# A two-block forward pass on one core: where a modulation's partial sums are given out, and which engine makes the second token tile's columns

## The chip, the cores and the metric

One Trainium2 chip, one of its cores. The program runs once per measurement, and the metric is the device time of the execution in microseconds (us). All weights come from HBM in float32; products are split into a high and a low part (`w_hi`, `w_lo`, and the same for activations), so that one float32 product is three products on TensorE (PE).

## What is computed

Two transformer-like blocks over 256 tokens of 1024 features. What matters here is the first block:

```python
def first_block(x, c, ctx, ...):
    mod_x = (silu(c) @ ada_w + ada_b)[:, None, :]
    sh1, sc1, g1, sh2, sc2, g2 = split(mod_x, 6, axis=-1)
    hx = modulate(rmsnorm(x, norm1_g), sh1, sc1)
    hc = modulate(rmsnorm(ctx, norm1_g), csh1, csc1)
    # pooled channels and neighbourhood attention (8 heads, with context)
    x = x + g1 * (concat([pool_x, attn_x]) @ w_out)
    h2 = modulate(rmsnorm(x, norm2_g), sh2, sc2)
    x = x + g2 * peer(h2, peer_wq, peer_keys, peer_u, peer_v)
    return rmsnorm(x, final_g)

def peer(h, w_q, sub_keys, u, v):      # per block of 128 tokens
    q = (xb @ w_q).reshape(tb, 8, 2, 128)
    s = einsum('thpd,hpnd->thpn', q, sub_keys)
    sv, si = top_k(s, 16)              # then the 16 best of 256 pairs
    a = gelu(einsum('td,thkd->thk', xb, u[experts]))
    return einsum('thk,thkd->td', g * a, v[experts])
```

The second block (`second_block`: a gated recurrence, a sparse attention and an MLP) follows.

## The kernel before

One class, `Net`, builds the whole program. The calls of all four compute engines go through one helper, so nearly every instruction stands under line 226 (L226) in the profile and is told apart by its tiles: PE is TensorE, DVE VectorE, ACT ScalarE, POOL GpSimd, SP SyncE (whose DMA queue loads the weights, 512 KB a block, into `w_raw`; ACT makes `w_hi` of it and DVE `w_lo`).

The order of the instructions on each engine is made when the program is built. Large products (`gemm_rows`, `gemm_cols`, and `product` for w_out) call `pump()` (L472) between their matmuls; `pump` gives out pieces of side work (generators) whose inputs it thinks are ready by its own estimates of cost. `until(mark)` pumps until a named piece has been given out, whether ready or not. On the chip each engine runs its own list in that order and waits with semaphores.

Inside the first block, in order: the value product (`ga` with w_hi of wi_v), then for b = 0 to 3 a query product and a keys product (wi_q, 128x256 outputs, and wi_k, 128x512 outputs, both `gc` in the trace), with the wi_pool product (`ga`) ahead of b = 3. When a keys product ends, `ev_k` (L964) splits it into `khl` (ACT, then one DVE subtraction) and starts the neighbourhood attention of two heads (`neighbours`: scores `s` on PE, `s` and `m` on DVE, `pr` on ACT, `prT` on PE, `pT` on ACT, `o` on PE, `rows` on ACT, `oT` on PE). Then comes w_out: 96 products `wo` in four steps of 24 (k2 = 0 to 3), whose result, gated by g1, is added to x.

The modulation vectors g1, sh2, sc2 and g2 are made beside this work. `mod_steps` (L734) makes one vector out of eight DVE steps: each multiplies a 128x1024 block of ada_w by a column and adds it into `msum` (the first is a TENSOR_SCALAR, the other seven are SCALAR_TENSOR_TENSOR), and then PE adds up `msum` over its partitions (`mr` for g1; eight `mc`, 16 records in the trace, for the three others). So there are 32 DVE steps, in this order: g1, sh2, sc2, g2. The blocks are `w_ada`, 512 KB each, loaded on POOL's DMA queue through a `Feed` (L189) that asks for two blocks ahead of use and has three buffers; the load for a later step is issued when the step that last read that buffer is done. `pump` gives out one step whenever PE's planned time has gone on by `pause` = 2.4 (`self.tick`). A new sum first forces the sum ahead of it to its end (`until(("msum", n - 1))`, L741), which also gives out whatever side work stands before it. Deadlines force what is left: `upto(1)` after the loop over b, `upto(3)` after k2 = 2, n = 0 of w_out (L1015), `upto(4)` ahead of k2 = 3 (L1018).

After w_out the first block's end makes the normed, scaled and shifted columns of both token tiles (`normed`, transposes `tp`, `xt`, then the split `hh` and `hl`), the first query product `q`, its transposes `q0t` and `q0T`. `peer` (L1148) then makes the first scores `sc`, DVE chooses the experts (MAX8 and what follows), and POOL issues 256 indirect gathers (`uv`, 1 MB each, nine buffers). For each, DVE makes a dot product, ACT the gate and a diagonal matrix, PE the product `va` into the output.

Of the kernel before, what the change touches and what calls it, by code (L numbers as in the profile page):

```python
# [9 lines left out]
F32 = mybir.dt.float32  # L10
# [9 lines left out]
D = 1024  # L20
# [249 lines left out]
class Net:  # L270
    def __init__(self, tc, I, out):
# [8 lines left out]
        self.wait, self.active, self.marks, self.ahead = [], [], Marks(self), None  # L280
        self.tick, self.pause, self.next = None, 0.0, 0.0
        self.rings, self.running, self.steps, self.ended = {}, [], {}, set()
# [189 lines left out]
    def pump(self):  # L472

        if self.tick and self.busy["pe"] >= self.next:
            self.next = self.busy["pe"] + self.pause
            self.tick()
        low = lambda: self.low < min(self.used + 2, self.high) and self.done["w", self.low][0] + HOP <= self.busy["pe"]
        if low():
            self.low_part()
        self.flush()  # L480
        while True:
            if low():
                self.low_part()
            if not self.step():
                break
# [293 lines left out]
    def first(self):  # L779
# [4 lines left out]
        with ExitStack() as es:  # L784
# [162 lines left out]
            for b in range(4):  # L947
# [16 lines left out]
                def ev_k(a, qs=qs, kh=kh, kl=kl, b=b):  # L964
                    self.parts(kh, kl, a)
                    for e in range(2):
                        for tt in range(2):
# [4 lines left out]
                self.gemm_cols(xh, xl, "wi_q", b, T, ev_q)  # L972
                load_bias(2 * b + 1)
                self.gemm_cols(xh, xl, "wi_k", b, 512, ev_k)
            self.flush()
# [54 lines left out]
            self.prepare(-1)  # L1030
            self.r2 = [self.small.tile([128, 1], F32, name="gr", tag="gr") for t in range(2)]
            y = [pool.tile([128, D], F32, name="normed", tag="normed", bufs=2) for t in range(2)]

            def scale(tt):
                v = self.small.tile([128, 1], F32, name="gv", tag="gv")
                nc.vector.scalar_tensor_tensor(v, ss[tt][:, 1:2], 1.0 / D, ss[tt][:, 0:1], op0=ALU.mult, op1=ALU.add)
                nc.gpsimd.tensor_tensor(self.r2[tt], v, self.nhalf[:, :1], op=ALU.pow)

            def turn(tt):
                ps = []  # L1040
                for h in range(2):
                    p = self.pt("tp").rearrange("p (i t) -> p i t", i=4)
                    for i in range(4):
                        k = 4 * h + i
                        nc.tensor.transpose(p[:, i], y[tt][:, k * 128:(k + 1) * 128], self.ident)
                    ps.append(p)
                return ps

# [21 lines left out]
            square(0, 1)  # L1070
            self.normed_by(y[0], 0)
            evac(1, 1)
            ps = turn(0)
            xt = shift(ps[0], 0, nc.scalar)
# [9 lines left out]
            for h in range(2):  # L1084
                wh, wl = self.block("wq0", h, held=1 + h, more=-h)
                for i in range(4):
                    k, c = 4 * h + i, slice(i * 256, i * 256 + 256)
                    self.mm3(a, self.hh[:, k, :128], self.hl[:, k, :128], wh[:, c], wl[:, c], k == 0, k == 7)
            self.normed_by(y[1], 1)
            ps = turn(1)  # L1090
            q = pool.tile([128, 256], F32, name="q0", tag="gx", bufs=2)
# [5 lines left out]
            nc.scalar.activation(self.q0T, p[:, :256].rearrange("p (i t) -> p i t", i=2), AF.Copy)  # L1097
            for h in range(2):
                both(1, h, shift(ps[h], h, nc.vector), nc.vector)()

# [47 lines left out]
    def peer(self):  # L1148
# [3 lines left out]
        with ExitStack() as es:  # L1152
# [209 lines left out]
            self.offload = -99.0  # L1362
            self.ahead = pool, 6, self.loaded
            sc0 = self.res.tile([128, 256], F32, name="sc0")
            p = self.pt("sc")
            score(p, lambda i: self.q0T[:, i], 0, self.keys0)
            nc.scalar.activation(sc0, p[:, :256], AF.Copy)
            st["scored"].add((0, 0))
            q = queries()
            while st["gathered"] < 8:  # L1370
                advance(0.1, 0)
            token_rows(0)
            for _ in range(4):
# [768 lines left out]
```

## Time and profile before

| what | us |
|---|---|
| median of three runs (lowest, highest) | 1526.38 (1524.91, 1527.83) |
| the profiled execution, its own time | 1531.74 |
| its span in the trace | 1530.0 |
| busy: PE, DVE, ACT, POOL | 1350.7, 1038.0, 715.8, 291.7 |

The span is what the profiler's records cover; the profiled execution's own time is 1.74 us more, and 5.36 us above the median of the runs. An engine's busy time is a sum over stages with different limits: the first block up to w_out takes the first 200 us, the gathers run from 221 to about 875, and the second block takes the rest.

### The profile page before, as it was taken

The numbers are of one execution on the slowest core, as the hardware profiler recorded it, in microseconds if no ns is written. First come the engines' busy times: TensorE is split into PE (matmuls) and PEld (weight loads), VectorE is DVE, ScalarE is ACT, GpSimd is POOL, SyncE is SP. The second block draws the span as 40 slices with busy tenths as digits, with TensorE's granted clock in tenths as the row PEclk, the third lists the DMA queues.
The fourth block names the chain that finished last, engine by engine and source line by source line (L and its number), as shares of the span: only waits on it lengthen the run. The fifth ranks groups of instructions, "written<-read, shape, count | busy, mean of one in ns | idle before, by whom it ended". The sixth has DMA issues, their size and how long they took to land.

```text
span 1530.0 us, 18426 instructions
## 1 busy us (share of the span) xinstructions
PE 1350.7 (88%) x5972; PEld 913.4 (60%) x5972; DVE 1038.0 (68%) x2240; ACT 715.8 (47%) x1670; POOL 291.7 (19%) x338
## 2 busy tenths in 40 slices
PE   7999968988998788777787789999999999999996
PEld 3787755544543233222222258978788887998874
DVE  5665778777777778666654467767667667776454
ACT  3443335444554545444433356566633655444443
POOL 2110123333333333333333200000000100000000
PEclk9998979999999999999999999999999999999998
DMA  9665659999999999999999934532333365655652
GB/s 344 237 221 187 206 196 419 418 419 418 420 418 420 419 420 418 420 420 419 420 421 419 405 116 161 182 111 83 97 124 125 114 191 164 188 186 184 189 165 100
DMA packets 82080, 420.19 MB, mean 275 GB/s; under 512 B 10336, under 2 KB 12928, under 8 KB 49088
## 3 DMA queue, kind: packets, MB, share of 16 engines
q0 software_dynamic: 42672, 289.22, 46.5%
q1 hardware_dynamic: 39024, 129.52, 25.8%
q8 instruction: 48, 0.79, 0.2%
q14 instruction: 48, 0.39, 0.1%
q10 hardware_dynamic: 288, 0.27, 0.1%
HBM read 417.93 MB, written 1.05 MB: 274 GB/s over the span
## 4 chain that ended last, share of the span: by engine, by line
PE 45%; DMA 28%; DVE 11%; ACT 6%; issue 5%; POOL 1%; SPq 0%; DVEq 0%; POOLq 0%; ACTq 0%
DMA uv<-in_uv,ids 25%; PE ga L226 19%; PE gc L226 9%; PE va L226 6%; DVE uv L226 3%; DVE w_lo L226 2%; PE hA L226 2%; PE wo L226 2%; PE s L226 2%; ACT w_hi L226 1%; PE o L226 1%; PE no L226 1%; POOL uv L1305 1%; ACT L226 1%; ACT nP L226 1%
## 5 line engine op out<-in xcount | busy, mean ns | idle before, releaser
L226 PE MATMUL va<-uv,diag 128*128 128x512 f32 x1024 | 504.4, 623 | 112.4 <-ACT diag L226 109.8
L226 DVE SCALAR_TENSOR_TENSOR uv<-uv,xr 128x1024 f32<-128x1024 f32 x256 | 311.8, 1219 | 195.7 <-DMA uv<-in_uv,ids 179.5
L226 PEld LDWEIGHTS va<-uv,diag 128*128 128x128 f32 x1024 | 180.4, 193 | 384.9 <-ACT diag L226 237.2
L226 DVE TENSOR_TENSOR w_lo<-w_raw,w_hi 128x1024 fp32r<-128x1024 f32 x217 | 264.4, 1222 | 141.0 <-ACT w_hi L226 140.9
L226 ACT ACTIVATE w_hi<-w_raw 128x1024 fp32r<-128x1024 f32 x217 | 229.0, 1059 | 221.2 <-PE ga L226 138.0
L1305 POOL DMA_INDIRECT uv<-in_uv,ids x256 | 246.8, 964 | 414.5 <-PE va L226 296.3
L226 ACT ACTIVATE ga<-dots 128x1 f32<-128x1 f32 x256 | 51.9, 203 | 339.8 <-DVE uv L226 334.4
L226 PE MATMUL gc<-hh,w_hi 128*128 128x256 f32 x520 | 175.3, 337 | 0.0
L226 PE MATMUL gc<-hh,w_lo 128*128 128x256 f32 x520 | 150.0, 289 | 11.7 <-DVE w_lo L226 11.7
L226 PE MATMUL gc<-hl,w_hi 128*128 128x256 f32 x520 | 149.9, 288 | 1.4 <-DVE hl L226 1.4
L226 PEld LDWEIGHTS gc<-hl,w_hi 128*128 128x128 f32 x520 | 102.5, 197 | 15.9 <-issue 14.2
L226 PEld LDWEIGHTS gc<-hh,w_hi 128*128 128x128 f32 x520 | 102.9, 198 | 14.3 <-issue 14.3
L226 PEld LDWEIGHTS gc<-hh,w_lo 128*128 128x128 f32 x520 | 102.4, 197 | 12.3 <-DVE w_lo L226 12.3
L226 ACT ACTIVATE diag<-ident,c 128x128 f32<-128x128 f32 x256 | 102.8, 402 | 8.4
L226 PE MATMUL ga<-w_hi,hh 128*128 128x512 f32 x240 | 100.3, 418 | 0.9 <-ACT w_hi L226 0.7
L226 PE MATMUL ga<-w_lo,hh 128*128 128x512 f32 x240 | 95.5, 398 | 3.8 <-DVE w_lo L226 3.7
L226 PE MATMUL ga<-w_hi,hl 128*128 128x512 f32 x240 | 95.5, 398 | 0.4 <-DVE hl L226 0.4
L226 ACT ACTIVATE c<-ga,g 128x1 f32<-128x1 f32 x256 | 75.4, 295 | 8.3
L226 POOL TENSOR_TENSOR gr<-gv,nhalf 128x1 f32<-128x1 f32 x8 | 5.1, 634 | 313.6 <-DVE gv L226 313.6
L226 PEld LDWEIGHTS ga<-w_lo,hh 128*128 128x128 f32 x240 | 46.1, 192 | 13.2 <-DVE w_lo L226 5.2
L226 PEld LDWEIGHTS ga<-w_hi,hl 128*128 128x128 f32 x240 | 45.9, 191 | 11.4 <-DVE hl L226 1.3
L226 PEld LDWEIGHTS ga<-w_hi,hh 128*128 128x128 f32 x240 | 46.2, 192 | 10.3 <-ACT w_hi L226 1.1
(428 smaller groups left out, 2057.9 us busy)
## 6 DMA issues: line engine op xcount, KB each, us to landing
w_ada<-in_ada POOLq DMA_DIRECT2D x32, 512.0 KB
w_raw<-in_w_up SPq DMA_DIRECT2D x32, 512.0 KB, 3.8
w_raw<-in_w_down SPq DMA_DIRECT2D x32, 512.0 KB, 3.5
w_raw<-in_wq SPq DMA_DIRECT2D x18, 512.0 KB, 7.8
ring<-in_ada SPq DMA_DIRECT2D x16, 512.0 KB, 9.5
w_raw<-in_w_kv SPq DMA_DIRECT2D x12, 512.0 KB, 3.9
w_raw<-in_w_out SPq DMA_DIRECT2D x8, 512.0 KB, 4.3
uv<-in_uv,ids POOLq DMA_INDIRECT x256
```

Source lines behind the costliest of these rows:

```text
L226: r = call(out, *args, **kwargs)
L1305: tc.nc.gpsimd.indirect_dma_start(rows[i], None, I["uv"], bass.IndirectOffsetOnAxis(ap=ids[i % 16], axis=0))
```

## The change

Two edits. First, a flag `hold`: it is set when a keys product begins and cleared in `ev_k` when its result is split, and while it is set `pump` gives out no modulation step. Steps that would have been given out there come at a later `pump`, or at a deadline. Second, the columns of the second token tile are no longer made at the end of the first block. They are made in `peer` behind the first scores: both halves of `xt` and `hh` on ACT (before: all of it on DVE), and the two `hl` on DVE after the eighth gather has been given out. `s2` and `sh2` are handed over in `self.cols2`; the transposes became a method, `turn8`; the tiles take other tags, and `r2` lies in a longer-lived pool.

```diff
--- before.py
+++ after.py
@@ -278,7 +278,7 @@
         self.busy, self.done, self.dma = dict(pe=0.0, dve=0.0, act=0.0, pool=0.0), {}, 0.0
         self.nsums = 0
         self.wait, self.active, self.marks, self.ahead = [], [], Marks(self), None
-        self.tick, self.pause, self.next = None, 0.0, 0.0
+        self.tick, self.pause, self.next, self.hold = None, 0.0, 0.0, False
         self.rings, self.running, self.steps, self.ended = {}, [], {}, set()
         self.depth, self.margin, self.backlog, self.offload, self.force = 4, 0.4, 2.5, -9.0, [False]
 
@@ -471,7 +471,7 @@
 
     def pump(self):
 
-        if self.tick and self.busy["pe"] >= self.next:
+        if self.tick and not self.hold and self.busy["pe"] >= self.next:
             self.next = self.busy["pe"] + self.pause
             self.tick()
         low = lambda: self.low < min(self.used + 2, self.high) and self.done["w", self.low][0] + HOP <= self.busy["pe"]
@@ -963,6 +963,7 @@
 
                 def ev_k(a, qs=qs, kh=kh, kl=kl, b=b):
                     self.parts(kh, kl, a)
+                    self.hold = False
                     for e in range(2):
                         for tt in range(2):
                             k = 2 * b + e, tt
@@ -971,6 +972,7 @@
 
                 self.gemm_cols(xh, xl, "wi_q", b, T, ev_q)
                 load_bias(2 * b + 1)
+                self.hold = True
                 self.gemm_cols(xh, xl, "wi_k", b, 512, ev_k)
             self.flush()
             upto(1)
@@ -1028,23 +1030,14 @@
             for n in range(2):
                 product(n, 1, 3, *ws[n])
             self.prepare(-1)
-            self.r2 = [self.small.tile([128, 1], F32, name="gr", tag="gr") for t in range(2)]
-            y = [pool.tile([128, D], F32, name="normed", tag="normed", bufs=2) for t in range(2)]
+            self.r2 = [self.res.tile([128, 1], F32, name=f"r2{t}") for t in range(2)]
+            y = pool.tile([128, D], F32, name="normed", tag="normed", bufs=2)
+            self.cols2 = s2, sh2
 
             def scale(tt):
                 v = self.small.tile([128, 1], F32, name="gv", tag="gv")
                 nc.vector.scalar_tensor_tensor(v, ss[tt][:, 1:2], 1.0 / D, ss[tt][:, 0:1], op0=ALU.mult, op1=ALU.add)
                 nc.gpsimd.tensor_tensor(self.r2[tt], v, self.nhalf[:, :1], op=ALU.pow)
-
-            def turn(tt):
-                ps = []
-                for h in range(2):
-                    p = self.pt("tp").rearrange("p (i t) -> p i t", i=4)
-                    for i in range(4):
-                        k = 4 * h + i
-                        nc.tensor.transpose(p[:, i], y[tt][:, k * 128:(k + 1) * 128], self.ident)
-                    ps.append(p)
-                return ps
 
             def shift(p, h, engine):
                 xt = pool.tile([128, 4, 128], F32, name="xt", tag="pr", bufs=3)
@@ -1068,9 +1061,9 @@
             scale(0)
             evac(0, 1)
             square(0, 1)
-            self.normed_by(y[0], 0)
+            self.normed_by(y, 0)
             evac(1, 1)
-            ps = turn(0)
+            ps = self.turn8(y)
             xt = shift(ps[0], 0, nc.scalar)
             low = both(0, 0, xt, nc.scalar)
             square(1, 1)
@@ -1086,8 +1079,6 @@
                 for i in range(4):
                     k, c = 4 * h + i, slice(i * 256, i * 256 + 256)
                     self.mm3(a, self.hh[:, k, :128], self.hl[:, k, :128], wh[:, c], wl[:, c], k == 0, k == 7)
-            self.normed_by(y[1], 1)
-            ps = turn(1)
             q = pool.tile([128, 256], F32, name="q0", tag="gx", bufs=2)
             nc.scalar.activation(q, a, AF.Copy)
             p = self.pt("q0t")
@@ -1095,8 +1086,15 @@
                 nc.tensor.transpose(p[:, i * 128:(i + 1) * 128], q[:, i * 128:(i + 1) * 128], self.ident)
             self.q0T = self.res.tile([128, 2, 128], F32, name="q0T")
             nc.scalar.activation(self.q0T, p[:, :256].rearrange("p (i t) -> p i t", i=2), AF.Copy)
-            for h in range(2):
-                both(1, h, shift(ps[h], h, nc.vector), nc.vector)()
+    def turn8(self, y):
+        ps = []
+        for h in range(2):
+            p = self.pt("tp").rearrange("p (i t) -> p i t", i=4)
+            for i in range(4):
+                k = 4 * h + i
+                self.nc.tensor.transpose(p[:, i], y[:, k * 128:(k + 1) * 128], self.ident)
+            ps.append(p)
+        return ps
 
     def normed_by(self, y, tt):
         nc = self.nc
@@ -1361,14 +1359,29 @@
 
             self.offload = -99.0
             self.ahead = pool, 6, self.loaded
+            s2, sh2 = self.cols2
             sc0 = self.res.tile([128, 256], F32, name="sc0")
             p = self.pt("sc")
             score(p, lambda i: self.q0T[:, i], 0, self.keys0)
             nc.scalar.activation(sc0, p[:, :256], AF.Copy)
             st["scored"].add((0, 0))
+            y = pool.tile([128, D], F32, name="y1", tag="g2r")
+            self.normed_by(y, 1)
+            ps = self.turn8(y)
+            xts = []
+            for h in range(2):
+                xt = pool.tile([128, 4, 128], F32, name="xt", tag=("vg", "qT")[h], bufs=1 + h)
+                for i in range(4):
+                    k = 4 * h + i
+                    nc.scalar.activation(xt[:, i], ps[h][:, i], AF.Identity, scale=s2[:, k:k + 1], bias=sh2[:, k:k + 1])
+                nc.scalar.activation(self.hh[:, 4 * h:4 * h + 4, 128:], xt, AF.Copy)
+                xts.append(xt)
             q = queries()
             while st["gathered"] < 8:
                 advance(0.1, 0)
+            for h in range(2):
+                c = slice(4 * h, 4 * h + 4)
+                nc.vector.tensor_tensor(self.hl[:, c, 128:], xts[h], self.hh.bitcast(F32)[:, c, 128:], op=ALU.subtract)
             token_rows(0)
             for _ in range(4):
                 next(q)
```

What moves, engine by engine. The first place is DVE at the end of the second keys product (b = 1). One piece of the difference there (- is before only):

```order
 L226 TENSOR_TENSOR w_lo<-w_raw,w_hi 128x1024 x2
 L226 SCALAR_TENSOR_TENSOR qs<-gc,qs 128x256
-L226 SCALAR_TENSOR_TENSOR msum<-w_ada,sl,msum 128x1024 x2
 L226 TENSOR_TENSOR khl<-gc,khl 128x512
 L226 TENSOR_TENSOR s<-s,bias 128x256
```

The two steps of a sum that stood ahead of `khl` are gone from this place.

The second place is DVE in w_out, towards its end, down to g2's `mc`. Before:

```order
L226 RECIPROCAL rz<-z 128x1
L226 TENSOR_TENSOR w_lo<-w_raw,w_hi 128x1024
L226 TENSOR_TENSOR s<-s,bias 128x256
L226 TENSOR_REDUCE m<-s 128x1
L226 SCALAR_TENSOR_TENSOR msum<-w_ada,sl,msum 128x1024
L226 SCALAR_TENSOR_TENSOR s_1339<-sc_294,n_112 128x8
L226 SCALAR_TENSOR_TENSOR msum<-w_ada,sl,msum 128x1024
L226 TENSOR_TENSOR w_lo<-w_raw,w_hi 128x1024
L226 SCALAR_TENSOR_TENSOR msum<-w_ada,sl,msum 128x1024
L226 RECIPROCAL rz<-z 128x1
L226 TENSOR_TENSOR ml<-oT,mh 128x256
L226 TENSOR_TENSOR g_85<-mc,adabc 128x8
```

Three steps of g2's sum stand here, with other work between them. And in the changed kernel, from the fourth step of sc2's sum to g2's `mc` (`sc_294` is sc2, `g_85` is g2):

```order
L226 TENSOR_TENSOR w_lo<-w_raw,w_hi 128x1024
L226 SCALAR_TENSOR_TENSOR msum<-w_ada,sl,msum 128x1024
L226 TENSOR_TENSOR w_lo<-w_raw,w_hi 128x1024
L226 SCALAR_TENSOR_TENSOR msum<-w_ada,sl,msum 128x1024 x4
L226 RECIPROCAL rz<-z 128x1
L226 TENSOR_TENSOR ml<-oT,mh 128x256
L226 TENSOR_TENSOR sc_294<-mc,adabc 128x8
L226 SCALAR_TENSOR_TENSOR s_1298<-sc_294,n_112 128x8
L226 TENSOR_SCALAR msum<-w_ada,sl 128x1024
L226 TENSOR_TENSOR w_lo<-w_raw,w_hi 128x1024
L226 SCALAR_TENSOR_TENSOR msum<-w_ada,sl,msum 128x1024 x7
L226 TENSOR_TENSOR g_85<-mc,adabc 128x8
```

The step that makes sc2 out of its `mc` stood ahead of all these rows before, at the first third of w_out. Now sc2's eight steps and g2's eight stand one behind the other, after sh2's `mc`, which itself now comes after the first 27 products of w_out (before: ahead of w_out). On PE, 12 products `wo` stand between sc2's `mc` and g2's, and 24 after g2's, which are k2 = 3; before, 60 products of w_out and some attention stood between the two.

The third place is ACT behind the first scores. In the changed kernel:

```order
L226 ACTIVATE sc_1748<-sc 128x256
L226 ACTIVATE y_1753<-x_107,r_1649 128x512
L226 ACTIVATE xt<-tp,sh_293,s_1298 128x128 x4
L226 ACTIVATE hh<-xt 128x4x128
L226 ACTIVATE xt<-tp,sh_293,s_1298 128x128 x4
L226 ACTIVATE hh<-xt 128x4x128
L226 ACTIVATE w_hi<-w_raw 128x1024 x3
```

Before, the copy `sc` was followed at once by the three `w_hi`, and the sixteen 128x128 operations and casts for the second tile stood on DVE (eight TENSOR_SCALAR, two CAST, two `hl`) ahead of the first MAX8. Now DVE has only its half of the second `normed` there, and the two `hl` behind the 256-wide `cand`.

## Rows read from the trace of the kernel before

**Rows 1.** The page, part 4: shares of the chain that ended last, by line.

```profile
DMA uv<-in_uv,ids 25%; PE ga L226 19%; PE gc L226 9%; PE va L226 6%; DVE uv L226 3%; DVE w_lo L226 2%; PE hA L226 2%; PE wo L226 2%; PE s L226 2%; ACT w_hi L226 1%; PE o L226 1%; PE no L226 1%; POOL uv L1305 1%; ACT L226 1%; ACT nP L226 1%
```

**Rows 2.** Windows (busy us and count of each engine, PEclk, DMA share, GB/s).

```profile
121.00:139.00 18.00, 15.43 (x60) 12.54 (x59) 6.92 (x14) 5.77 (x13) 1.06 (x2) 0.62 0.32 96
...
192.00:200.00 8.00, 7.87 (x30) 6.04 (x29) 4.75 (x9) 2.41 (x6) 0.37 (x1) 0.79 0.21 68
...
600.00:870.00 270.00, 213.32 (x434) 74.50 (x432) 163.44 (x362) 107.42 (x337) 102.89 (x109) 0.99 1.01 420
```

**Rows 3.** Timeline of PE (start, length, operation, idle before and releaser): keys product.

```profile
72.47 0.49 PE L226 MATMUL s<-khl,qs 64*128 64x512 f32 x1 [0.69 <-ACT khl L226]
75.55 2.50 PE L226 MATMUL s<-khl,qs 64*128 64x512 f32 x5 [2.59 <-DVE khl L226]
...
80.49 0.38 PE L226 MATMUL gc<-xh,w_lo 128*128 128x256 f32 x1
80.70 0.28 PE L226 MATMUL gc<-xh,w_hi 128*128 128x256 f32 x1
```

**Rows 4.** Timeline of DVE at the same place.

```profile
72.30 2.60 DVE L226 SCALAR_TENSOR_TENSOR msum<-w_ada,sl,msum 128x1024 f32<-128x1024 f32 x2
```

**Rows 5.** Timeline of PE, inside the wi_pool product.

```profile
123.31 1.10 PE L226 MATMUL o<-vr,pT 128*128 128x64 f32 x8 [0.75 <-ACT pT L226]
125.49 1.12 PE L226 MATMUL prT<-ident,pr 128*128 128x128 f32 x4 [1.07 <-ACT pr L226]
127.35 1.97 PE L226 MATMUL o<-vr,pT 128*128 128x64 f32 x8 [0.75 <-ACT pT L226]
129.11 3.52 PE L226 MATMUL mc<-ones,msum 128*128 128x1 f32 x16
```

**Rows 6.** Timeline of PE, w_out.

```profile
159.89 0.40 PE L226 MATMUL wo<-w_hi,mh 128*128 128x512 f32 x1
...
162.70 1.84 PE L226 MATMUL mc<-ones,msum 128*128 128x1 f32 x16
...
190.79 1.84 PE L226 MATMUL mc<-ones,msum 128*128 128x1 f32 x16
192.49 0.48 PE L226 MATMUL wo<-w_hi,mh 128*128 128x512 f32 x1
```

**Rows 7.** Timeline of DVE, w_out.

```profile
164.66 0.75 DVE L226 TENSOR_SCALAR msum<-w_ada,sl 128x1024 f32<-128x1024 f32 x1
...
176.58 1.22 DVE L226 TENSOR_TENSOR w_lo<-w_raw,w_hi 128x1024 fp32r<-128x1024 f32 x1 [0.85 <-ACT w_hi L226]
...
182.88 0.43 DVE L226 TENSOR_TENSOR s<-s,bias 128x256 f32<-128x256 f32 x1
...
183.95 1.27 DVE L226 SCALAR_TENSOR_TENSOR msum<-w_ada,sl,msum 128x1024 f32<-128x1024 f32 x1
185.15 0.16 DVE L226 SCALAR_TENSOR_TENSOR s<-sc,n 128x8 f32<-128x8 f32 x1
```

**Rows 8.** Timeline of POOL, w_out: one load of a modulation block.

```profile
165.70 0.53 POOL L226 DMA_DIRECT2D w_ada<-in_ada  x1 [3.13 <-DVE msum L226]
```

**Rows 9.** The page, part 6 (KB each, us from issue to landing).

```profile
w_raw<-in_w_out SPq DMA_DIRECT2D x8, 512.0 KB, 4.3
```

**Rows 10.** Chain of waits (start, length, what), in the first sums.

```profile
61.83 6.58 DMA w_ada<-in_ada
```

**Rows 11.** Timeline of DVE between the first block and the gathers.

```profile
210.84 1.37 DVE L226 TENSOR_SCALAR xt<-tp,s,sh 128x128 f32<-128x128 f32 x4 [2.34 <-PE tp L226]
...
215.78 0.29 DVE L226 MAX8 sv<-sc 128x8 f32<-128x128 f32 x1
```

**Rows 12.** Timeline of ACT at the same place.

```profile
212.68 0.39 ACT L226 ACTIVATE sc<-sc 128x256 f32<-128x256 f32 x1 [0.80 <-PE sc L226]
...
226.49 0.21 ACT L226 ACTIVATE g<-g 128x16 f32<-128x16 f32 x1 [10.59 <-DVE g L226]
```

**Rows 13.** Timeline of POOL: the first gather.

```profile
221.02 1.05 POOL L1305 DMA_INDIRECT uv<-in_uv,ids  x1 [11.31 <-DVE sv L226]
```

## The prediction, made before the changed kernel ran

> **What bounds the kernel now.** I began with the chain that ended last. A quarter of the span on it is the gathers themselves [rows 1]; so I looked next at the windows, for the state of the DMA engines in that stretch. From 600 to 870 us they are full: share 1.01, 420 GB/s, while PE, DVE and ACT all have idle time [rows 2]. A gather is 128 rows of 8 KB, 1.05 MB, and 1.05 MB at 420 GB/s are 2.5 us; 256 of them are 640 us. Nothing that the change does to the engines inside this stretch can shorten it, and it moves no bytes. What counts is when the first gather is issued, 221.02 [rows 13]: a shift of it goes one for one to the end (at the least to nothing, if the first few gathers are not yet bound by DMA; I take one for one, since the stretch is full for hundreds of us). The whole question is therefore the path through the first 221 us, which runs over PE's products, waits of PE for DVE and ACT, and the half clock that follows such waits. I read that from the timelines of PE, DVE and POOL.
>
> **What the first edit gains.** (a) At the end of the second keys product DVE runs two steps of a sum, 2.60 us, ahead of the subtraction `khl` [rows 4], and PE waits 2.59 us for that [rows 3]. After the wait PE's clock is at half: five `s` take 2.50, twice their full-speed time (1.25 lost), and the products behind them stand at 0.21 from start to start until 80.70 and at about half of it afterwards, 1.3 more. With no step given out there, all of it goes: 2.59 + 1.25 + 1.3 = 5.1. At the least it is 2.6 (if the half clock came anyway), at the most 5.1.
>
> (b) Inside the wi_pool product, sc2's first step forces sh2's sum out early, and with it attention pieces whose inputs are not there: PE waits 0.75, 1.07 and 0.75 [rows 5], which are all of its 2.57 idle us from 121 to 139. The mean granted clock is 0.62 there [rows 2]: (1 - 0.62) x 2 x 18 = 13.7 us at half clock, of which some 11.9 are busy, so 5.9 are lost. In the changed order nothing is forced there. Gain 2.6 + 5.9 = 8.5; at the least the 2.6, at the most 9.4, if the steps' fill times go too.
>
> (c) sh2's `mc`, 1.8 at full clock [rows 6], moves behind the start of w_out. So w_out starts 5.1 + 8.5 + 1.8 = 15.4 us sooner, at 159.9 - 15.4 = 144.5 [rows 6].
>
> **What the first edit costs.** The steps held back are not dropped. Sixteen of the 32, all of sc2 and g2, now stand behind sh2's `mc`, and the last 24 products of w_out stand behind g2's. Before, only three steps of g2's stood late in w_out, and PE had products to do beside them. The new path, from sh2's `mc` on:
> - Until sh2's `mc`, PE has 27 products at 0.234 (12 of them from 159.89 to 162.70 [rows 6]), 6.3; nine `s` at 0.25, 2.3; three groups of `prT`, 1.2, and three of `o`, 2.5; and two waits for `pT` like those in [rows 5], 1.5. Together 13.8: sh2's `mc` starts at 158.3.
> - Then DVE alone sets the pace. sc2's half: `mc` 1.7, sh2 0.2, the first step 0.67 (164.66 to the next instruction), seven steps at 1.20 (183.95 to 185.15), 8.4 [rows 7]; three `w_lo` at 1.14 (1.22 less the overlap), 3.4; one `s` with its `m`, 1.07 (182.88 to 183.95) [rows 7]: 15.5. Attention's `rz` and `ml`, 0.4. g2's half: `mc` 1.7, sc2 and s2 0.25, 0.67, one `w_lo` 1.14, seven steps 8.4: 12.1. One wait of a `w_lo` for its `w_hi`, 0.8 [rows 7]. Sum 28.8.
> - Then the loads. There are three buffers, so step k + 3 waits for a load that POOL issues when step k has ended, 0.29 after it (164.66 + 0.75 to 165.70, [rows 7, 8]). The trace before has no burst of steps, so how long a `w_ada` takes in one must be bounded: the nearest 512 KB load is w_out's, 4.3 [rows 9]; the chain shows a `w_ada` of 6.58 in the first sums [rows 10]; and below, nothing is waited for if a load takes no more than 3.2, since three steps take 3.6. I take 4.3, the load that runs at this very time. Three steps then need 1.2 + 0.3 + 4.3 + 0.1 = 5.9 instead of 3.6. The first three of a burst find their blocks loaded; walking through the sixteen, sc2's half waits 2.3 and g2's 4.6. Sum 6.9.
> - PE meanwhile runs dry. Until sc2's `mc` it has some 13 us of work in 18, until g2's 12 products, 2.8 us, in some 18. A wait of 1 us was enough to bring half clock in [rows 5]. `mc` takes 3.52 at half clock [rows 5] and 1.84 at full [rows 6]: 1.7 for sc2's, 1.7 for g2's.
>
> So g2's `mc` starts at 158.3 + 28.8 + 6.9 + 1.7 = 195.7 instead of 190.79 [rows 6]: 4.9 later, and it takes 1.7 more. Of the last 24 products some ran at half clock before, too: 0.79 over the 8 us from 192 is 3.4 us at half [rows 2], 1.7 lost. After the wait in [rows 5] half clock lasted almost 10 us from the `mc`; less its 3.5, some 6 us would fall on the products, 3 lost: 1.3 more (bounds -1.7 with no half clock, +3.9 with all 24 in it). First edit: 4.9 + 1.7 + 1.3 = +7.9.
>
> **The rule beside it.** The profile has no `w_ada` alone; its nearest row says 4.3. The Trainium skill, page "DMA: Bandwidth & Descriptors", section "Anatomy of one DMA — SWDGE (gpsimd) path", fits a transfer as 2.0 us plus its bytes over 436 GB/s, an estimated 3.2 us for 512 KB; by that the term of 6.9 would be nothing. No row here shows a load that short, and 4.3 and 6.58 speak against it where other loads run.
>
> **What the second edit does.** Before, DVE makes the second tile's columns from 210.84 until the first MAX8 at 215.78 [rows 11]; the scores that MAX8 reads were copied at 212.68 + 0.39 = 213.07 [rows 12]. Without that work MAX8 starts at 213.1: 2.7 sooner, and the first gather with it (bounds: nothing, if the scores come later; 4.9, all the work that left). ACT gets it, about 5 us ahead of its three `w_hi`; it had 10.6 us of idle time before its next need at 226.49 [rows 12], so that is covered. The two `hl`, 1.3 us, now stand ahead of two `w_lo` on DVE and delay the second choice, which was moved 2.7 sooner; and eight gathers, 20 us of DMA, lie in front of it. If that cover were gone it would cost the 1.3. I count nothing.
>
> **Sum.** +7.9 - 2.7 = +5.2. The profiled execution took 1531.74, so its like would be 1536.9; it stood 5.4 above the median of the runs, 1526.38, and I forecast for the median: **1531.6**. A measurement of this kernel tells 0.2%, 3.05 us, from no change.
>
> **Rivals.**
> - *The loads keep pace: faster.* Place: the two bursts. If a `w_ada` lands within 3.2 us of its issue, the 6.9 goes, and since loads of w_out then land sooner as well, the 0.8 for `w_hi`; the gap ahead of g2's `mc` shrinks by 4.6 and I take away the 1.3 of clock: -9.0, 1522.6. This decides from 3.2 us down. For: from 192 to 200 the DMA share is 0.21 [rows 2], so there is room. Against: 4.3 and 6.58 [rows 9, 10]. The rule of the Trainium skill's page named above is this rival's. 0.14.
> - *The clock holds: no change.* If PE's clock stays up through the dry stretch, both `mc` and the last products cost 4.7 less: 1526.9. For: `mc` at 162.70 and 190.79 ran at full clock, the second right after waits for attention. Against: the `mc` behind 1 us waits at 129.11 did not. 0.25.
> - *The loads are as slow as in the chain: worse.* With 6.58 three steps take 8.2 us; walking through the sixteen gives 8.9 more: 1540.5. For: 6.58 was on the path once. Against: it was in a stretch with more loads. 0.11.
> - *My sum*, within its bounds 1528.5 to 1535: 0.50.
>
> From these: faster 0.14, within 0.2% 0.25, slower 0.61. The range takes in the first rival's time and leaves out the slowest: 1522.5 to 1538.
>
> **What would show it.** Right: no wait for `khl` and full clock behind the second keys product; w_out's first `wo` near 144; then DVE rows of `msum` with idle time released by DMA w_ada; g2's `mc` near 196 with 3.5 us; MAX8 released by ACT's `sc`; the first gather near 226 (221.0 + 5.2); the gather stretch as long as before. Wrong: g2's `mc` before 191, or `msum` steps back to back at 1.2, or a gather stretch that changes in length.

## The result, and the profile after

The changed kernel took 1534.83 us (median of seven runs, 1532.29 to 1540.76) against 1526.38 (seven runs): the ratio is 1.0057, 95% interval 1.0036 to 1.0078, so it is 5.5 to 12 us slower. Forecast: 1531.6, slower with a chance of 0.61, range 1522.5 to 1538. The profiled execution, 1540.76, is the longest of its seven; a second profile of the same kernel stands among the experiments.

From the page after, the span and the chain's shares by line:

```profile
span 1539.0 us, 18431 instructions
...
DMA uv<-in_uv,ids 28%; PE ga L226 18%; PE gc L226 9%; DVE uv L226 3%; PE va L226 3%; DVE w_lo L226 2%; PE hA L226 2%; DMA w_ada<-in_ada 1%; PE s L226 1%; ACT w_hi L226 1%; PE o L226 1%; PE no L226 1%; POOL uv L1303 1%; ACT nP L226 1%; ACT diag L226 1%
```

The gathers' DMA has 3 points more of the chain than in [rows 1], and `va`, which stands in the same stretch, 3 less. The stretch is as full as in [rows 2], and from the first gather to the last `va` it is 667.5 us against 669.2 before. Windows (columns as there):

```profile
72.00:90.00 18.00, 16.76 (x74) 13.59 (x75) 11.40 (x20) 6.67 (x14) 1.06 (x2) 0.72 0.63 185
95.00:108.00 13.00, 12.09 (x51) 9.54 (x51) 5.99 (x11) 4.53 (x10) 0.53 (x1) 0.74 0.36 104
121.00:139.00 18.00, 18.00 (x102) 14.63 (x101) 13.24 (x21) 10.53 (x20) 2.11 (x4) 1.00 0.71 220
...
192.00:206.00 14.00, 2.86 (x10) 1.94 (x9) 9.54 (x8) 1.06 (x1) 2.44 (x5) 0.62 0.65 225
600.00:870.00 270.00, 211.94 (x431) 74.64 (x429) 166.69 (x373) 111.34 (x346) 101.79 (x107) 0.99 1.01 419
```

Two things stand in them. From 121 to 139, where the kernel before had a clock of 0.62, PE is now busy without a gap at 1.00. But from 72 to 90 and from 95 to 108 the clock is 0.72 and 0.74, and from 192 to 206 PE is busy for 2.9 of 14 us. PE at the first two keys products (where the first answers to [rows 3]):

```profile
72.36 0.50 PE L226 MATMUL s<-khl,qs 64*128 64x512 f32 x1 [0.69 <-ACT khl L226]
73.74 2.35 PE L226 MATMUL s<-khl,qs 64*128 64x512 f32 x5 [0.88 <-DVE khl L226]
...
96.47 0.50 PE L226 MATMUL s<-khl,qs 64*128 64x512 f32 x1 [0.69 <-ACT khl L226]
97.19 1.14 PE L226 MATMUL s<-khl,qs 64*128 64x512 f32 x3 [0.23 <-DVE khl L226]
```

DVE's two steps no longer stand between, but ACT's part of `khl` (0.69) and DVE's (0.88) are still waited for, half clock follows, and it now also follows the next keys product, which in the kernel before had other work behind it. One word in what stands ahead of this section was wrong: the keys product that ends at 72 is the first (b = 0), not the second.

So nothing is gained up to the wi_pool product. Its first product, before and after, and the stretch from the first query product to it:

```profile
113.43 0.39 PE L226 MATMUL ga<-w_hi,xh 128*128 128x512 f32 x1
118.99 0.48 PE L226 MATMUL ga<-w_hi,xh 128*128 128x512 f32 x1
```

```profile
63.05:113.43 50.38, 46.92 (x265) 38.70 (x264) 36.26 (x51) 20.57 (x43) 6.89 (x13) 0.93 0.71 237
63.05:118.99 55.94, 53.46 (x272) 43.86 (x270) 28.36 (x45) 21.97 (x45) 3.17 (x6) 0.85 0.55 170
```

It begins 5.6 us later. From there to w_out it is 33.5 us instead of 46.5: 13.0 gained, of which 1.0 is a group of eight `o` that now stands ahead of wi_pool.

PE in w_out, which answers to [rows 6]: the first product and sh2's `mc`, and then the `oT` ahead of sc2's `mc`, that `mc`, g2's, and the first of the last 24 products:

```profile
152.48 0.40 PE L226 MATMUL wo<-w_hi,mh 128*128 128x512 f32 x1
...
166.26 1.90 PE L226 MATMUL mc<-ones,msum 128*128 128x1 f32 x16
```

```profile
186.76 0.48 PE L226 MATMUL oT<-ident,rows 128*128 128x128 f32 x1 [6.87 <-ACT rows L226]
187.03 3.41 PE L226 MATMUL mc<-ones,msum 128*128 128x1 f32 x16
...
205.89 3.54 PE L226 MATMUL mc<-ones,msum 128*128 128x1 f32 x16 [11.14 <-DVE msum L226]
209.30 0.77 PE L226 MATMUL wo<-w_hi,mh 128*128 128x512 f32 x1
```

w_out starts 7.4 us sooner, and g2's `mc` 15.1 us later. In between, DVE waits for the loads, which [rows 7] had nothing of (DVE's timeline, the steps that wait):

```profile
182.38 1.28 DVE L226 SCALAR_TENSOR_TENSOR msum<-w_ada,sl,msum 128x1024 f32<-128x1024 f32 x1 [1.76 <-DMA w_ada<-in_ada]
184.94 1.28 DVE L226 SCALAR_TENSOR_TENSOR msum<-w_ada,sl,msum 128x1024 f32<-128x1024 f32 x1 [1.27 <-DMA w_ada<-in_ada]
...
195.64 1.28 DVE L226 SCALAR_TENSOR_TENSOR msum<-w_ada,sl,msum 128x1024 f32<-128x1024 f32 x1 [0.49 <-DMA w_ada<-in_ada]
199.05 1.28 DVE L226 SCALAR_TENSOR_TENSOR msum<-w_ada,sl,msum 128x1024 f32<-128x1024 f32 x1 [2.13 <-DMA w_ada<-in_ada]
200.88 2.63 DVE L226 SCALAR_TENSOR_TENSOR msum<-w_ada,sl,msum 128x1024 f32<-128x1024 f32 x2 [0.54 <-DMA w_ada<-in_ada]
204.46 1.29 DVE L226 SCALAR_TENSOR_TENSOR msum<-w_ada,sl,msum 128x1024 f32<-128x1024 f32 x1 [0.95 <-DMA w_ada<-in_ada]
```

The view of the tile `w_ada` from 150 to 215 sums it up: DVE's idle time ahead of a step, with the number of waits, and the time from issue to landing of the loads.

```profile
  DMA w_ada<-in_ada: 7.1, 6
...
DMA to landing us min/median/max: 3.7/4.3/5.3
```

Then the columns. DVE's first MAX8, against [rows 11]; and POOL's first gather, against [rows 13]:

```profile
230.07 0.29 DVE L226 MAX8 sv<-sc 128x8 f32<-128x128 f32 x1 [4.25 <-ACT sc L226]
```

```profile
235.31 1.05 POOL L1303 DMA_INDIRECT uv<-in_uv,ids  x1 [9.14 <-PE xr L226]
```

MAX8 now waits for ACT's copy of the scores. The first gather is issued 14.3 us later than before.

### The profile page after: what moved, and what is told of

It is laid out like the page before. It is cut to its first block, busy times and chain, and to the rows that moved or that the text cites. A ratio compares the mean times of both kernels' runs of the same rounds, so it can differ in the third digit from the quotient of the medians.

```text
span 1539.0 us, 18431 instructions
## 1 busy us (share of the span) xinstructions
PE 1352.6 (88%) x5972; PEld 917.5 (60%) x5972; DVE 1034.2 (67%) x2230; ACT 719.3 (47%) x1680; POOL 292.7 (19%) x338
## 4 chain that ended last, share of the span: by engine, by line
PE 40%; DMA 31%; DVE 12%; issue 7%; ACT 5%; POOL 1%; SPq 0%; DVEq 0%; POOLq 0%; ACTq 0%
DMA uv<-in_uv,ids 28%; PE ga L226 18%; PE gc L226 9%; DVE uv L226 3%; PE va L226 3%; DVE w_lo L226 2%; PE hA L226 2%; DMA w_ada<-in_ada 1%; PE s L226 1%; ACT w_hi L226 1%; PE o L226 1%; PE no L226 1%; POOL uv L1303 1%; ACT nP L226 1%; ACT diag L226 1%
## 5 line engine op out<-in xcount | busy, mean ns | idle before, releaser
L226 PEld LDWEIGHTS gc<-hh,w_hi 128*128 128x128 f32 x520 | 103.6, 199 | 15.3 <-issue 14.2
```

What stands on the lines that cost most here:

```text
L226: r = call(out, *args, **kwargs)
```

## The experiments

The theory: the sums' steps that the hold keeps back are made one behind the other in w_out, and PE waits for them; the columns gain about 3. The rivals: the columns on ACT are the loss; the hold costs by what happens at the keys products; the loads land in time. All ratios are to the kernel before on the same chip.

**Only the columns.** The changed kernel without

```diff
-                self.hold = True
```

> Only the second edit (the second tile's columns behind the first scores), no hold. My theory (columns gain, the held-back sums cost): 2.7 to 3.1 us faster than the kernel before, first gather near 218, everything up to w_out's end as in the kernel before. Rival (ACT's new work delays what follows, or the gathers' stretch takes the gain back): no difference or slower than the kernel before.

Measured 1524.95 us, ratio 0.9980 (0.9958 to 1.0001): 3.1 us faster, with an interval that just reaches no change. The first MAX8 in its profile:

```profile
212.53 0.29 DVE L226 MAX8 sv<-sc 128x8 f32<-128x128 f32 x1 [4.24 <-ACT sc L226]
```

The first gather is issued at 217.77, 3.25 sooner. The rival falls: the loss isn't the columns'.

**Only the hold.** The kernel before with the flag and nothing of the columns:

```diff
-        if self.tick and self.busy["pe"] >= self.next:
+        if self.tick and not self.hold and self.busy["pe"] >= self.next:
...
                     self.parts(kh, kl, a)
+                    self.hold = False
...
+                self.hold = True
                 self.gemm_cols(xh, xl, "wi_k", b, 512, ev_k)
```

> Only the first edit (no step of the modulation while a keys product runs), columns as before. My theory: 11 to 12 us slower than the kernel before, since the changed kernel's +8.5 already holds a gain of about 3 from the columns; g2's mc near 206. Rival (the loss comes from the columns on ACT): no slower than the kernel before.

Measured 1544.23, ratio 1.0094 (1.0066 to 1.0121): 10 to 18.5 us slower, and g2's `mc` at 201.2, where 206 was expected. The first gather is at 232.6. So the whole loss is the hold's, somewhat more than expected.

**The hold, with the steps twice as close outside of it.**

```diff
-                self.tick, self.pause, self.next = step, 2.4, self.busy["pe"] + 2.4
+                self.tick, self.pause, self.next = step, 1.2, self.busy["pe"] + 2.4
```

> The changed kernel with the pause between steps at 1.2 instead of 2.4: still no step while a keys product runs, but outside of them the steps come twice as close. sh2's mc then stands ahead of w_out and sc2's after 15 products instead of 27 and 60; g2's stays after 72. My theory (the cost is the sixteen steps one behind the other in w_out): the loss goes, 0 to 4 us faster than the kernel before. Rival (the cost is what the hold does at the keys products, waits for khl and half clock): still 4 us or more slower than the kernel before.

Measured 1548.59, ratio 1.0121 (1.0096 to 1.0145): the slowest of all, against the theory as I had put it. The number is the rival's, but not its cause: the waits for `khl` at the first keys product are 0.69 and 0.22. PE's waits elsewhere in its profile:

```profile
76.29 3.75 PE L226 MATMUL mr<-msum,ones 128*128 128x512 f32 x4 [6.05 <-DVE msum L226]
...
131.96 0.66 PE L226 MATMUL prT<-ident,pr 128*128 128x128 f32 x4 [2.06 <-ACT pr L226]
```

The first sum's `mr` waits 6.05 us for its steps (which themselves wait for their loads, 2.31 and 2.13), and at 132 and 138.7, as in [rows 5], attention pieces are forced out whose inputs are not there. w_out starts at 172.7. Steps given out too early cost as well: a sum that begins forces the one ahead of it, and what stands before that. What was missing in my theory is this other side.

**No hold, but a longer pause.** The columns moved, and:

```diff
-                self.tick, self.pause, self.next = step, 2.4, self.busy["pe"] + 2.4
+                self.tick, self.pause, self.next = step, 3.4, self.busy["pe"] + 2.4
...
-                self.hold = True
```

> No hold, but the pause between steps at 3.4 instead of 2.4, with the columns moved: the steps come late although none is held back; sc2's mc stands after 57 products of w_out, g2's after 72. My theory (late sums cost, whatever makes them late): 5 to 12 us slower than the columns alone, so 2 to 9 us slower than the kernel before. Rival (only the hold at the keys products costs): as the columns alone, 2 to 3 us faster than the kernel before.

Measured 1524.80, ratio 0.9970 (0.9951 to 0.9989): as the columns alone, as the rival said. But the trace does not say that late steps are free. w_out starts at 145.7, 14.2 us sooner than before, for the forced pieces are gone (the window that has 0.62 in [rows 2]):

```profile
121.00:139.00 18.00, 18.00 (x120) 16.06 (x119) 11.12 (x20) 9.10 (x19) 1.59 (x3) 1.00 0.71 220
```

and PE then waits for g2's last steps:

```profile
186.98 3.55 PE L226 MATMUL mc<-ones,msum 128*128 128x1 f32 x16 [14.23 <-DVE msum L226]
```

At g2's `mc`, 3.8 of the 14.2 are left (187.0 against 190.8). Whether a late step costs is a question of how many there are, which the runs below tell.

**The changed kernel once more.**

> The changed kernel itself once more, beside runs of the kernel before on this chip, and for a second profile: its first profile is of its longest run. Expected 8 to 10 us slower than the kernel before. If w_out starts at 147 in it, as it did in the kernel with the hold alone, whose program is the same up to there, then the start at 152.5 in the first profile was the clock's chance behind the keys products; if it starts at 152 again, the columns have a part in it.

Measured 1534.55, ratio 1.0041 (1.0021 to 1.0061). In its profile w_out starts at 149.7, g2's `mc` at 203.0 and the first gather at 232.4: 3 us sooner than in the first profile, with the same program. PE behind the first keys product, and the windows there:

```profile
74.80 0.50 PE L226 MATMUL s<-khl,qs 64*128 64x512 f32 x1 [0.69 <-ACT khl L226]
75.53 1.44 PE L226 MATMUL s<-khl,qs 64*128 64x512 f32 x5 [0.23 <-DVE khl L226]
```

```profile
72.00:90.00 18.00, 17.09 (x100) 13.55 (x98) 13.02 (x22) 8.89 (x20) 1.59 (x3) 1.00 0.71 234
95.00:108.00 13.00, 13.00 (x53) 10.09 (x53) 7.06 (x12) 6.36 (x14) 0.53 (x1) 0.74 0.53 141
```

The waits are 0.69 and 0.23 here, and the clock stays at 1.00 from 72 to 90, against 0.72 in the first profile; it falls from 95 to 108 in both. In the kernel with the hold alone, the same program up to there, w_out starts at 147.4. So 147 to 152.5 is chance, the first profile is at its bad end, and the columns have no part in it. But it is not all behind the keys products. The second profile's first query product begins 2.45 us later than the first's, 65.52 against 63.07, behind a stretch with half clock (the first profile, then the second):

```profile
30.00:40.00 10.00, 8.65 (x43) 5.83 (x42) 7.36 (x13) 5.37 (x8) 0.57 (x1) 1.00 0.68 232
30.00:40.00 10.00, 9.26 (x33) 5.58 (x32) 5.83 (x11) 2.88 (x5) 0.57 (x1) 0.67 0.62 222
```

From that query product to w_out it is 89.4 us in the first profile, and 84.2 and 84.3 in the second and with the hold alone. DVE's wait of 0.88 in the first has a reason of its own: the step given out ahead of the product waited longer for its load (first profile, then hold alone), and `khl` stands behind that step.

```profile
69.19 1.29 DVE L226 SCALAR_TENSOR_TENSOR msum<-w_ada,sl,msum 128x1024 f32<-128x1024 f32 x1 [2.83 <-DMA w_ada<-in_ada]
68.81 1.28 DVE L226 SCALAR_TENSOR_TENSOR msum<-w_ada,sl,msum 128x1024 f32<-128x1024 f32 x1 [2.18 <-DMA w_ada<-in_ada]
```

**Without the late loads.** Blocks from the twentieth on are not loaded; their steps read a block that is there. The sums, and with them the rows that are gathered, are then others.

```diff
-            w = self.tile(len(self.blocks))
-            (self.engine or self.net.nc.sync).dma_start(w, self.net.I[name][tuple(at)])
+            w = (again := name == "ada_2" and len(self.blocks) >= 19) and self.blocks[-3] or self.tile(len(self.blocks))
+            again or (self.engine or self.net.nc.sync).dma_start(w, self.net.I[name][tuple(at)])
```

> The changed kernel without the loads of the last thirteen of the 32 modulation blocks: their steps read blocks that are already there (the last sums are made of earlier blocks of ada_w), so no step of the two bursts waits for a load. My theory (the loads' landings are 7 of the loss): 6 to 8 us faster than the changed kernel, about 1 us slower than the kernel before. Rival (DVE or PE set the pace of the bursts, loads land in time): as the changed kernel.

Measured 1532.16, ratio 1.0024 (1.0002 to 1.0046), against 1.0041 for the changed kernel beside it: 2.6 us less by the ratios instead of 6 to 8, and the intervals overlap, so the size in the whole time is not settled. In the trace the steps run back to back, DVE first, and from sh2's `mc` to g2's PE takes 34.2 us instead of 39.6 and 39.4:

```profile
174.08 5.24 DVE L226 SCALAR_TENSOR_TENSOR msum<-w_ada,sl,msum 128x1024 f32<-128x1024 f32 x4
...
185.65 9.21 DVE L226 SCALAR_TENSOR_TENSOR msum<-w_ada,sl,msum 128x1024 f32<-128x1024 f32 x7
```

```profile
160.84 2.02 PE L226 MATMUL mc<-ones,msum 128*128 128x1 f32 x16
...
195.00 3.54 PE L226 MATMUL mc<-ones,msum 128*128 128x1 f32 x16 [7.22 <-DVE msum L226]
```

So without the loads the burst is 5.3 us shorter, though the waits for them were 7.1: some comes back as waits of `w_lo` for `w_hi`, 1.38 and 0.82 where the changed kernel had 0.66 and 0.18. The remaining 34 are DVE's work and these waits, with `mc` and its half clock.

**The hold at one keys product, b = 1.**

```diff
-                self.hold = True
+                self.hold = b == 1
```

> The changed kernel with the hold at the second keys product alone (b = 1, where the subtraction waited behind two steps). 20 steps instead of 14 are then done ahead of w_out; sh2's mc stands ahead of w_out, sc2's after 57 products. My theory (it is the number of steps left for w_out that costs): 8 to 12 us faster than the changed kernel, so at or up to 3 us below the kernel before. Rival (holding at a keys product costs by itself): half of that at the most.

Measured 1529.84, ratio 1.0013 (0.9994 to 1.0031): 4.3 us less than the changed kernel beside it by the ratios. That is less than my 8 to 12 and within the rival's half, so the time alone does not decide. The hold was aimed at the wrong product: the wait at the first is untouched,

```profile
75.86 2.50 PE L226 MATMUL s<-khl,qs 64*128 64x512 f32 x5 [2.99 <-DVE khl L226]
```

but with 20 steps instead of 14 ahead of w_out, 4.3 of the changed kernel's 6.3 us are gone, though the intervals overlap.

**Two paces.** Columns moved; pause 3.0, and 1.4 from w_out on.

```diff
-                self.tick, self.pause, self.next = step, 2.4, self.busy["pe"] + 2.4
+                self.tick, self.pause, self.next = step, 3.0, self.busy["pe"] + 2.4
...
-                self.hold = True
...
             upto(1)
+            self.pause, self.next = 1.4, self.busy["pe"]
```

> No hold, columns moved, the pause 3.0 up to w_out and 1.4 from there on: few steps between the keys products, and the rest spread over w_out (mc of sc2 after 39 products, g2's after 72). If both findings hold (steps ahead of w_out force attention pieces too early, steps behind its middle make PE wait), this has w_out's early start near 146 without the 14 us of PE's wait for the last sum: 4 to 10 us faster than the columns alone, 8 to 14 faster than the kernel before. Rival (the DVE's total sets the pace whatever the spread): as the columns alone.

Measured 1525.54, ratio 0.9987 (0.9972 to 1.0001): a miss, no better than the columns alone. w_out starts at 145.5, but the last steps still hold `rz` and so the attention's last `oT`, and `mc` runs at half clock (3.41 for all 16 records; the row, cut at 190, has twelve):

```profile
187.41 0.48 PE L226 MATMUL oT<-ident,rows 128*128 128x128 f32 x1 [4.61 <-ACT rows L226]
187.68 2.56 PE L226 MATMUL mc<-ones,msum 128*128 128x1 f32 x12
```

**The hold at the first keys product alone, where the wait was.** 

```diff
-                self.hold = True
+                self.hold = b == 0
```

> The changed kernel with the hold at the first keys product alone (b = 0; it is the one that ends at 72, so the texts so far call it wrongly the second, and the hold at b = 1 did not reach it). 24 of the 32 steps are done ahead of w_out as in the kernel before, mc of sh2, sc2 and g2 stand after 0, 12 and 72 products. My theory: the wait for khl at 72 falls from 2.6 to 0.5 to 0.9, no steps are left over for w_out, so 0 to 4 us faster than the columns alone. Rival (half clock behind the keys products comes with any such wait, however short): no difference to the columns alone.

Measured 1525.49, ratio 0.9984 (0.9969 to 0.9999); the wait for DVE falls to 0.45,

```profile
73.27 1.42 PE L226 MATMUL s<-khl,qs 64*128 64x512 f32 x5 [0.45 <-DVE khl L226]
```

and the first gather is issued at 215.6, 2.2 sooner than with the columns alone. In the whole time the two can't be told apart. The products behind the wait begin 3.0 us sooner (74.6 against 77.7), but w_out only 0.6 (159.1 against 159.7): at the next keys product PE waits 1.23 and 0.23 for `khl`, and the clock from 90 to 104 is 0.88 against 1.00. The other 1.5 at the first gather come from the last 24 products, which ran without half clock in this profile. The hold at this product costs nothing where no steps are left over, and gains little.

**The last steps out of w_out.** The two paces, and g2's last three steps after the first tile's columns, its `mc` behind `q0T`:

```diff
-            upto(4)
             self.tick = None
             self.drain()
...
             scale(1)
+            upto(4)
...
             nc.scalar.activation(self.q0T, p[:, :256].rearrange("p (i t) -> p i t", i=2), AF.Copy)
+            self.drain()
```

> The kernel with two paces (no hold, pause 3.0 and then 1.4, columns moved), and in addition g2's last three steps given out after the first tile's columns and its mc behind q0T, so that nothing of w_out waits for them (g2 is first read by the gathers' gate, far later). My theory (PE's last wait in w_out is for these steps): the last 24 products start near 183 instead of 191, mc costs 2 to 3.5 ahead of the scores, so 3 to 6 us faster than the two paces alone and 5 to 9 faster than the kernel before. Rival (PE waits for attention there anyway, or the steps now hold up the scores): as the two paces.

Measured 1523.44, ratio 0.9977 (0.9965 to 0.9989): 1.7 to 5.3 us faster than the kernel before, and as good as any other here (pause 3.4 has 0.9970, and the intervals overlap). PE and POOL:

```profile
182.38 0.33 PE L226 MATMUL oT<-ident,rows 128*128 128x128 f32 x1 [0.29 <-ACT rows L226]
...
201.22 2.43 PE L226 MATMUL mc<-ones,msum 128*128 128x1 f32 x16 [0.63 <-DVE msum L226]
```

```profile
210.41 1.05 POOL L1304 DMA_INDIRECT uv<-in_uv,ids  x1 [5.35 <-PE xr L226]
```

The wait ahead of `oT` is 0.29 instead of 4.61, `mc` takes 2.43 ahead of the scores, and the first gather is 7.0 us sooner than with the two paces. Of that the runs show 1.5 by the ratios, within the intervals, and the two spans are 1520.4 and 1520.2 us: in the profiles nothing of the 7.0 is left at the end. From the first gather to the last `va` it is 671.0 us instead of 667.7, and behind that 639.0 instead of 635.1.

**The kernel before, once more.**

> The kernel before once more, for a second profile of it: how far do two profiles of one program differ, up to the first gather and behind it? In the first one the first gather stands at 221.0, and 1309 us lie from it to the end of the span, against 1304 in both profiles of the changed kernel, whose PE order is the same from there on. If those 5 us are chance, this profile lies elsewhere than 1309, between 1302 and 1310; if the columns give something back behind the first gather, it is 1309 again. First gather expected within 2 us of 221.

The first gather is at 221.65, 0.63 from the first profile. From there to the end of the span it is 1308.8 us, again 1309. Up to there the two differ by more: w_out starts at 162.4 instead of 159.9, and g2's `mc` at 191.8 instead of 190.8.

**What the runs say together.** By the program's order, the number of steps that stand behind w_out's start, and the time from w_out's first product to g2's `mc` in the profiles (not in it: the two with loads left out or g2 moved, and the run with steps twice as close, which takes 44.7 with as many steps in that stretch as the kernel before, as PE waits 7.0 there for attention):

| kernel | steps left | first `wo` | first `wo` to g2's `mc` |
|---|---|---|---|
| before, two profiles | 8 | 159.9; 162.4 | 30.9; 29.4 |
| columns only; hold at b = 0 | 8; 8 | 159.7; 159.1 | 30.9; 30.9 |
| hold at b = 1 | 12 | 154.5 | 39.0 |
| pause 3.4; two paces | 13; 13 | 145.7; 145.5 | 41.3; 42.2 |
| changed, two profiles | 18 | 152.5; 149.7 | 53.4; 53.2 |
| hold only | 18 | 147.4 | 53.7 |

The stretch of the kernel before and of the changed kernel:

```profile
159.89:190.79 30.90, 29.86 (x152) 23.91 (x151) 23.24 (x31) 13.06 (x23) 3.71 (x7) 0.94 0.69 234
152.48:205.89 53.41, 34.11 (x167) 27.72 (x166) 34.34 (x41) 14.33 (x25) 7.91 (x15) 0.79 0.60 207
```

From 8 to 18 steps it is 22.5 us more. PE's idle time is 18.3 of them (1.0 before, 19.3 after), and 1.9 is sh2's `mc`, which stands in this stretch only with 18. Without that `mc` it is some 2 us a step, and from 8 to 12 or 13 steps 2.0 to 2.3: 1.2 of it are DVE's own, the loads are 5.3 us of the whole, and half clock and the attention held up behind the steps were not measured apart. The kernel with pause 3.4 pays 10.4 for five steps and has 14.2 of w_out's earlier start; the changed kernel pays 22.5 for ten and has 7.4 and 10.2, and 12.5 with the hold alone.

## Why the prediction was right, point by point

- *The keys product (gain 5.1).* This is the step that failed. wi_pool was to begin 5.1 sooner, and began 5.6 later in the first profile and 2.8 in the second (118.99 and 116.21 against 113.43; the second profile of the kernel before has 115.53). Of that 1.0 is the group of `o` that moved ahead of it, and in the second profile 2.3 were lost before the first query product. DVE's wait fell from 2.59 to 0.88 and 0.23 us, but "with no step given out there, all of it goes" took the half clock to go with it. ACT's part of `khl` alone keeps PE waiting, and half clock came at 72 in one profile and at 96 in both, where the kernel before had none at 96. I had looked at one keys product, and not at what the changed order puts behind the next.
- *The wi_pool product (8.5, and 1.8 for sh2's `mc`).* Right in its cause: no wait and full clock from 121 to 139. In size 13.0 from wi_pool's start to w_out's, or 12.0 without the `o` that moved, against 10.3.
- *w_out's start.* Forecast 144.5; 152.5 and 149.7. The sum of gains was 15.4 and measured 7.4 and 10.2: 13.0 less the 5.6 and 2.8 of the first term.
- *sh2's `mc` to g2's.* Forecast 158.3 to 195.7, 37.4 us; measured 39.6 and 39.4. The landing time taken from w_out's row, 4.3, is the median of the burst's own loads, 3.7 to 5.3. The waits for loads were forecast at 6.9; the view of the tile has 7.1, and the burst is 5.3 shorter when the loads go.
- *The rule of the Trainium skill, "DMA: Bandwidth & Descriptors"*, section "Anatomy of one DMA — SWDGE (gpsimd) path", would have given an estimated 3.2 for such a load and no wait. The trace does not agree, and it decides: none of these loads, beside others, landed in less than 3.7.
- *Half clock.* `mc` was forecast at 3.5 and took 3.41 and 3.54. Of the last 24 products I had 1.3 more than before; from g2's `mc` to the last product it is 10.9 against 8.7, of which 1.7 is `mc`: 0.5.
- *The columns (2.7).* Right: in the run with the columns alone, the first gather is 3.25 sooner. From the last query product to MAX8 it is 2.5 us in the changed kernel and 5.6 before.
- *The gathers carry the shift one for one.* From the first gather to the last `va` it is 669.2 and 667.5 in the two profiles before and 667.5 and 668.7 after: right within 2 us. But from the first gather to the end of the span the profiles with the old columns have 1309.0, 1308.8 and 1310.0 us, and nine of the ten with the columns moved 1301.9 to 1306.3 (the tenth, with g2's late steps, has 1310.0); most of that lies behind the last `va`. The hold alone and the second profile of the changed kernel show it best: they issue the first gather at 232.6 and 232.4 and end at 1542.6 and 1536.3. PE's order is the same there, but the waits on DMAs that the program sets are partly others. No run tells which, so the cause stays open. In timed runs the columns alone gain 3.1 (-0.2 to 6.4), which neither asks for it nor excludes it. And where g2's late steps brought the first gather 7.0 sooner, the end did not follow.

So the cost of the held-back steps was forecast well, from its mechanism, but that the sum came so near is luck in part. The +5.2 against +8.45 (5.5 to 12) has two errors against each other: the first gather was forecast at 226.2 and came at 232.4 and 235.3, chiefly for the first term, and some 5 us came back behind the first gather, which nothing in the forecast had. The rival with loads that keep pace fell with the landings; the one with the clock fell with `mc` at 3.4 and 3.5; the one with 6.58 a load fell too.

## What to carry to other kernels

Work that is kept out of a busy place must be made somewhere: before holding it back, count the pieces that will be left at the next deadline, and price them with the engine's own time plus its loads (some 2 us for a step of 1.2 here). Removing the wait for one of two producers, DVE here, leaves the other's, and half clock can follow that too: here it came behind waits of 0.69 and 0.88 us in one profile. And a sum that no one reads for long (g2) need not end in the stage in which it was begun, though an earlier start of the next stage, as here, need not reach the end of the program.

## What the runs showed of the hardware that was not expected

One program, two profiles: behind waits of 0.69 and 0.88 us the granted clock was 0.72 from 72 to 90, behind waits of 0.69 and 0.23 it was 1.00. From the first query product to w_out's start the two differ by 5.2 us (89.4 and 84.2), for that and what follows. The two profiles of the kernel before differ by 2.5 at w_out's start. One profile of a kernel can't tell a gain of this size; the table above can tell 18 steps from 8, since that stretch takes 53.2 to 53.7 in three profiles and 29.4 to 30.9 in four.
